# A fixed order for the first product of a decoder layer: small loads, transposes and splits placed by hand

## The chip, the cores and the metric

The kernel runs on one core of one Trainium2 chip. The metric is the device time of one execution in microseconds (us); the profile's span, from the first to the last instruction of the profiled execution, is a little shorter. Engines are named as the profile names them: PE (TensorE matmuls), PEld (its weight loads), DVE (VectorE), ACT (ScalarE), POOL (GpSimd), SP (SyncE, which here only issues DMAs).

## The reference: one layer of a hybrid trunk

For one sequence of 256 positions with 2048 channels, float32:

```
x = x + 1/2 * SwiGLU_1(RMSNorm(x))          # w_gate, w_up: 2048 x 5632, w_down: 5632 x 2048
x = x + mixer(RMSNorm(x))                   # three token mixers, w_in 2048 x 5120, w_out 2048 x 2048
x = x + 1/2 * SwiGLU_2(RMSNorm(x))
out = RMSNorm(x)
swiglu(h, wg, wu, wd) = (silu(h @ wg) * (h @ wu)) @ wd
```

## The kernel before

All large products run as three matmuls per block: the stationary operand is x (or h) transposed, split into a high and a low part in a reduced float32 format (`xh`, `xl`), the moving operand is a weight tile, split the same way (`wh`, `wl`), and PE sums hi·wh, lo·wh and hi·wl. The 256 positions are two tiles of 128 rows (t = 0, 1), the 2048 channels are 16 blocks k of 128, and outputs are made in columns of 512. So one k costs 6 matmuls of 512 columns, and one product over all 16 k costs 96. Weights come over SP's queue into `wt` (4 buffers, up to four k per load, 1 MB); ACT rounds `wt` to `wh`, DVE makes `wl = wt - wh` (3 buffers each).

The first product, `ag` (x times the first 512 columns of w_gate), is special, because x itself has to be brought in first. `first_block` (L528) runs ahead of each load of weights that begins a new group of four k: it loads the next 512 channels of x, PE turns them (`tp`, L230: 8 transposes of 128x128 into two banks of PSUM), and for each of the four k in it ACT writes `xh` (L252, with the norm's gain from `prm`) and DVE writes `xl` (L253), both reading `tp`. The loads of weights are cut 1, 1, 2, 4, 4, 4. `prm` comes from a small load and one transpose (`pp`, L87). At the very start 14 transposes of the identity (`spin`, L101) keep PE occupied while nothing has landed.

The order on each engine is not that of the text: a list scheduler, which works with a model of durations, places every instruction, and the weight splits of the ordinary `gemm` have a raised priority. The product `au` (the same x times w_up) follows `ag`.

Of the kernel before, what the change touches and what calls it, by code (L numbers as in the profile page):

```python
# [1 line left out]

# [6 lines left out]
F32 = mybir.dt.float32  # L9
F32R = mybir.dt.float32r  # L10
# [6 lines left out]
P = 128  # L17
NB = 512
# [6 lines left out]
def hybrid_trunk(ctx, tc, x, ffn1_norm, ffn1_w_gate, ffn1_w_up, ffn1_w_down, mix_norm, w_in,  # L25
# [31 lines left out]
    xr = [pool.tile([P, T, NB], F32, name=f"x{n}") for n in range(DN)]  # L57
    xv = x[0].rearrange("(t p) d -> p t d", p=P)

    def load_x(n):  # L60
        nc.sync.dma_start(out=xr[n], in_=xv[:, :, n * NB:(n + 1) * NB])


    small, col = [], {}
# [7 lines left out]
    NP = sum(r.shape[0] for r in small)  # L72
    prm = pool.tile([P, NP], F32, name="prm")

    def load_params(which, at):
        n = sum(r.shape[0] for r in which)
        rows = pool.tile([n, P], F32, name="rows", tag="rows", bufs=1)
        r0 = 0
        for v in which:
            nc.scalar.dma_start(out=rows[r0:r0 + v.shape[0], :], in_=v)  # L80
            r0 += v.shape[0]
        return rows, at, n

# [3 lines left out]
        nc.tensor.transpose(pp[:, :n], rows, ident[:n, :n])  # L87
        nc.vector.tensor_copy(out=prm[:, at:at + n], in_=pp[:, :n])

    first_params = load_params(small[:1], 0)  # L90
    load_x(0)
    ident = pool.tile([P, P], F32, name="ident")
    make_identity(nc, ident)
    mhalf = pool.tile([P, T], F32, name="mhalf")
# [1 line left out]

    early = pool.tile([P, T], F32, name="early")
    nc.scalar.activation(out=early, in_=mhalf, func=AF.Silu)
    spin = tp_tile("spin")
    for i in range(14):  # L100
        nc.tensor.transpose(spin[:, :P], ident, ident)  # L101
    place_params(first_params)

# [31 lines left out]


    high = [None]
    later = []  # L140

    def gemm(lhs, w, n0, ks, name, cuts=None, before=None, by_tile=None):

        def bank_pair():
            return psum.tile([P, T, NB], F32, name=name, tag="acc", bufs=2)

        acc = bank_pair()  # L150
        acc_of = [acc] * T
        if by_tile:
            acc_of = [acc] + [bank_pair() for _ in range(T - 1)]
        nk = len(ks)
        c0 = 0
        held = []

        def products(t, c0, kk, wh, wl):
            ts = slice(t * P, (t + 1) * P)
            for i, k in enumerate(kk):  # L160
                hi, lo = lhs(k)
                first, last = c0 + i == 0, c0 + i == nk - 1
                acc = acc_of[t]
                nc.tensor.matmul(acc_of[t][:, t, :], lhsT=hi[:, ts], rhs=wh[:, i, :], start=first, stop=False)  # L164
                nc.tensor.matmul(acc_of[t][:, t, :], lhsT=lo[:, ts], rhs=wh[:, i, :], start=False, stop=False)  # L165
                nc.tensor.matmul(acc_of[t][:, t, :], lhsT=hi[:, ts], rhs=wl[:, i, :], start=False, stop=last)  # L166

        cuts = cuts or [CH] * (nk // CH)
        for ci, m in enumerate(cuts):
            kk = ks[c0:c0 + m]  # L170
            if before:
                before(kk[0])
            wt = stat.tile([P, CH, NB], F32, name="wt", tag="wt", bufs=4)
            nc.sync.dma_start(
                out=wt[:, :m],
                in_=w[kk[0] * P:(kk[-1] + 1) * P, n0:n0 + NB].rearrange("(k p) n -> p k n", p=P))
            wh = stat.tile([P, CH, NB], F32R, name="wh", tag="wh", bufs=3)
            wl = stat.tile([P, CH, NB], F32R, name="wl", tag="wl", bufs=3)
            with nullcontext() if before else tc.high_priority():
                high[0] = nc.scalar.activation(out=wh[:, :m], in_=wt[:, :m], func=AF.Copy)  # L180
                nc.vector.tensor_sub(out=wl[:, :m], in0=wt[:, :m], in1=wh[:, :m].bitcast(F32))  # L181
            if by_tile and ci >= len(cuts) - 3:
                held.append((c0, kk, wh, wl))
            else:
                for i, k in enumerate(kk):
                    for t in range(T):
                        products(t, c0 + i, [k], wh[:, i:i + 1], wl[:, i:i + 1])
            c0 += m
            step()
        if by_tile:  # L190
            for t in range(T):
                for h in held:
                    products(t, *h)
                by_tile(t, acc_of[t])
        return acc
# [46 lines left out]
                                    in_=sv[a * Q:(a + 1) * Q, :, :, j, :])  # L242
        return dst

    def gained(n, c0, at_once=False):

        tp = transposed(xr[n]) if at_once else turned(xr[n], work([P, 4, S], "xt"))
        hi = stat.tile([P, 4, S], F32R, name="xh", tag="xh", bufs=4)
        lo = stat.tile([P, 4, S], F32R, name="xl", tag="xl", bufs=4)
        for i in range(4):  # L250
            g = prm[:, c0 + 4 * n + i:c0 + 4 * n + i + 1]
            nc.scalar.activation(out=hi[:, i, :], in_=tp[:, i, :], func=AF.Copy, scale=g)  # L252
            nc.vector.scalar_tensor_tensor(out=lo[:, i, :], in0=tp[:, i, :], scalar=g,  # L253
                                           in1=hi[:, i, :].bitcast(F32), op0=ALU.mult,
                                           op1=ALU.subtract)
        return hi, lo
# [16 lines left out]
                                           in1=xr[n][:, t, :], op0=ALU.mult, op1=ALU.add)  # L273


    def ffn(xt, rs, wg, wu, wd, after, cuts=None, before=None, last_tile=None):

        ht = {}  # L280

        def hidden(j, **first):
            ag = gemm(block_of(xt), wg, j * NB, range(KD), "ag", **first)
# [24 lines left out]
            later.append(turn)  # L308

        for j0 in range(0, FB, 6):  # L310
            js = range(j0, min(j0 + 6, FB))
            for j in js:
                hidden(j, **(dict(cuts=cuts, before=before) if j == 0 else {}))
            ks = range(4 * js[0], 4 * js[-1] + 4)
            done = js[-1] == FB - 1
            for n in range(DN):
                if done and n == DN - 1 and last_tile:
                    def tile_done(t, acc, n=n):
                        residual(acc, n, 0.5, [t])
                        last_tile(t)  # L320
                    gemm(block_of(ht), wd, n * NB, ks, "ad", by_tile=tile_done)
                    continue
                acc = gemm(block_of(ht), wd, n * NB, ks, "ad")
                residual(acc, n, 0.5)
                if done:
                    after(n)


    def mixer(l, xt, rs_of, after):
# [1 line left out]
        rs = rs_of()  # L331
        cc, cp = col["conv", l], col["ps", l]
        pw = pool.tile([P, 4, P], F32, name="pw", tag="pw", bufs=1)
        nc.scalar.dma_start(out=pw, in_=pool_w[l].rearrange("g c d -> c g d"))
        DA = D // 2
        off = {"q": 0, "k": DA, "v": 2 * DA, "b": 3 * DA, "c": 3 * DA + NB, "u": 3 * DA + 2 * NB,
               "p": 3 * DA + 3 * NB}
# [187 lines left out]

    ss0, xt, r0 = new_stats(), {}, []

    def first_block(k):  # L528
        if k % 4 == 0:
            n = k // 4  # L530
            if n:
                load_x(n)
            xt[n] = gained(n, col["ffn1", 0], at_once=True)

    def first_rs():
        if not r0:
            r0.append(rstd_of(ss0))
            more = load_params(small[1:], small[0].shape[0])
            later.extend([lambda: place_params(more), masks, pool_consts])
        return r0[0]  # L540

# [38 lines left out]

    rs = first_rs
    for l in range(DEPTH):
        start = dict(cuts=[1, 1, 2, 4, 4, 4], before=first_block) if l == 0 else {}
        x1, r1 = phase("mix", l, lambda a: ffn(xt, rs, ffn1_w_gate[l], ffn1_w_up[l], ffn1_w_down[l],
                                               a, **start))
# [36 lines left out]
```

## Time and profile before

| what | value |
|---|---|
| median of three runs | 1793.72 us (1793.63 to 1793.86) |
| the profiled execution's own time | 1793.22 us |
| its span | 1791.1 us |
| PE busy | 1776.9 us, 99% |
| DVE, ACT busy | 64%, 42% |
| first matmul of `ag` starts | 8.87 us |
| `ag` and `au` are both through, the next `ag` starts | 58.08 us |

PE is occupied nearly throughout, so the span is read as a chain of PE work, with the few stretches in which PE waits; those lie in the first 20 us. [...]

### The profile page before, as it was taken

The page shows a single profiled execution, that of the slowest core. Times are in us where ns is not written, and L with a number is a line of the kernel's source. Part 1 is how long each engine was busy: PE and PEld are TensorE (multiplying, and loading weights), DVE is VectorE, ACT ScalarE, POOL GpSimd, SP SyncE. Part 2 cuts the span into 40 slices and gives each one's busy share as a digit, 9 for nine tenths or more (in the row PEclk, how much of TensorE's full clock was granted, in tenths as well). Part 3 has the DMA queues.
Part 4 walks back from the last instruction along what each step waited for, and adds up shares of the span by engine and source line. Part 5 has one row for each costly group of instructions (what it writes and reads, how often), then busy time and mean ns, then how long its engine had stood idle before and what let it go on. Part 6 is the DMA issues. An engine that isn't in the chain of part 4 may idle for free.

```text
span 1791.1 us, 19137 instructions
## 1 busy us (share of the span) xinstructions
PE 1776.9 (99%) x7928; PEld 1464.4 (82%) x7928; DVE 1144.3 (64%) x1260; ACT 748.6 (42%) x598; POOL 5.5 (0%) x19
## 2 busy tenths in 40 slices
PE   8999999999999999999999999999999999999998
PEld 7888888888888888887778888888888888888886
DVE  5766666444666687768767896666664446666653
ACT  6434433333344344545544455443443334433342
POOL 0000000000000000000000000000000000000000
PEclk9999999999999999999999999999999999999999
DMA  8655555555555555554545555555556555555652
GB/s 289 211 189 196 199 192 188 190 201 196 188 190 198 198 181 195 197 199 146 188 141 188 167 207 190 188 188 194 198 197 209 189 189 196 199 191 188 218 197 78
DMA packets 172262, 342.32 MB, mean 191 GB/s; under 512 B 5456, under 2 KB 6032, under 8 KB 172176
## 3 DMA queue, kind: packets, MB, share of 16 engines
q1 hardware_dynamic: 171232, 339.76, 56.2%
q10 hardware_dynamic: 944, 1.34, 0.3%
q8 instruction: 62, 1.02, 0.2%
q14 instruction: 24, 0.20, 0.0%
HBM read 338.98 MB, written 2.10 MB: 190 GB/s over the span
## 4 chain that ended last, share of the span: by engine, by line
PE 98%; DVE 1%; DMA 0%; ACT 0%; issue 0%; ACTq 0%; POOLq 0%
PE au L164 9%; PE ad L166 9%; PE au L165 9%; PE ad L164 9%; PE au L166 9%; PE ad L165 9%; PE ag L166 9%; PE ag L164 9%; PE ag L165 9%; PE az L164 4%; PE az L166 4%; PE az L165 4%; PE ao L166 1%; PE ao L165 1%; PE ao L164 1%; DVE wl L181 0%
## 5 line engine op out<-in xcount | busy, mean ns | idle before, releaser
L181 DVE TENSOR_TENSOR wl<-wt,wh 128x2048 fp32r<-128x2048 f32 (+1 forms) x322 | 732.8, 2277 | 543.4 <-ACT wh L180 541.4
L180 ACT ACTIVATE wh<-wt 128x2048 fp32r<-128x2048 f32 (+1 forms) x322 | 613.6, 1905 | 867.0 <-PE au L165 281.3
L164 PE MATMUL ag<-wh,xh 128*128 128x512 f32 x704 | 274.8, 390 | 2.1 <-ACT xh L252 2.1
L165 PE MATMUL ag<-wh,xl 128*128 128x512 f32 x704 | 274.6, 390 | 0.3 <-DVE xl L253 0.3
L166 PE MATMUL ag<-wl,xh 128*128 128x512 f32 x704 | 274.5, 390 | 0.2 <-DVE wl L181 0.2
L164 PE MATMUL au<-wh,xh 128*128 128x512 f32 x704 | 274.0, 389 | 0.0
L165 PE MATMUL au<-wh,xl 128*128 128x512 f32 x704 | 273.9, 389 | 0.0
L166 PE MATMUL au<-wl,xh 128*128 128x512 f32 x704 | 273.9, 389 | 0.0
L165 PE MATMUL ad<-wh,hl 128*128 128x512 f32 x704 | 273.9, 389 | 0.0
L164 PE MATMUL ad<-wh,hh 128*128 128x512 f32 x704 | 273.9, 389 | 0.0
L166 PE MATMUL ad<-wl,hh 128*128 128x512 f32 x704 | 273.7, 389 | 0.0
L241 DVE STREAM_TRANSPOSE ht<-h 32x256 f32<-32x256 f32 x352 | 153.5, 436 | 5.6
L164 PEld LDWEIGHTS ag<-wh,xh 128*128 128x128 f32 x704 | 132.4, 188 | 29.7 <-ACT xh L252 2.4
L166 PEld LDWEIGHTS ag<-wl,xh 128*128 128x128 f32 x704 | 132.5, 188 | 28.0 <-DVE wl L181 0.6
L165 PEld LDWEIGHTS ag<-wh,xl 128*128 128x128 f32 x704 | 132.4, 188 | 28.1 <-DVE xl L253 0.8
L165 PEld LDWEIGHTS ad<-wh,hl 128*128 128x128 f32 x704 | 132.2, 188 | 27.5
L164 PEld LDWEIGHTS au<-wh,xh 128*128 128x128 f32 x704 | 132.2, 188 | 27.5
L166 PEld LDWEIGHTS au<-wl,xh 128*128 128x128 f32 x704 | 132.2, 188 | 27.4
L166 PEld LDWEIGHTS ad<-wl,hh 128*128 128x128 f32 x704 | 132.2, 188 | 27.4
L165 PEld LDWEIGHTS au<-wh,xl 128*128 128x128 f32 x704 | 132.2, 188 | 27.3
L164 PEld LDWEIGHTS ad<-wh,hh 128*128 128x128 f32 x704 | 132.2, 188 | 27.3
L164 PE MATMUL az<-wh,xh 128*128 128x512 f32 x320 | 126.8, 396 | 0.0
(116 smaller groups left out, 1142.1 us busy)
## 6 DMA issues: line engine op xcount, KB each, us to landing
wt<-in_ffn_w_up_dram SPq DMA_DIRECT2D x88, 1024.0 KB, 5.1
wt<-in_ffn_w_down_dram SPq DMA_DIRECT2D x88, 1024.0 KB, 5.1
wt<-in_ffn_w_gate_dram SPq DMA_DIRECT2D x87, 1024.0 KB, 5.1
wt<-in_w_in_dram SPq DMA_DIRECT2D x40, 1024.0 KB, 5.0
wt<-in_w_out_dram SPq DMA_DIRECT2D x16, 1024.0 KB, 5.1
x<-in_x_dram SPq DMA_DIRECT2D x4, 512.0 KB, 10.3
out_dram<-xg SPq DMA_DIRECT2D x8, 256.0 KB, 3.1
gf<-in_final_norm_dram ACTq DMA_DIRECT2D x2, 512.0 KB, 4.7
```

The costliest lines, as they stand in the source:

```text
L164: nc.tensor.matmul(acc_of[t][:, t, :], lhsT=hi[:, ts], rhs=wh[:, i, :], start=first, stop=False)
L165: nc.tensor.matmul(acc_of[t][:, t, :], lhsT=lo[:, ts], rhs=wh[:, i, :], start=False, stop=False)
L166: nc.tensor.matmul(acc_of[t][:, t, :], lhsT=hi[:, ts], rhs=wl[:, i, :], start=False, stop=last)
L180: high[0] = nc.scalar.activation(out=wh[:, :m], in_=wt[:, :m], func=AF.Copy)
L181: nc.vector.tensor_sub(out=wl[:, :m], in0=wt[:, :m], in1=wh[:, :m].bitcast(F32))
L241: nc.vector.transpose(out=dv[j * Q:(j + 1) * Q, :, :, a, :], in_=sv[a * Q:(a + 1) * Q, :, :, j, :])
```

## The change

The scheduler no longer orders the first product. A new function `opening` writes it out by hand, under a manual schedule:

- x comes in five loads (the first 512 channels as two halves), and the first product's weights in loads of one or two k, all in a written order; a further load is issued where a buffer comes free.
- The first 14 idle transposes are followed, after the transposes of the first half of the first x load, by five more.
- `prepare(n)` (8 transposes) and `ready(n)` (the four `xh`, `xl`) of x's block n stand ahead of the products of k = 4n - 1, and the split of the weights for k = 4n stands behind those products in the text.
- Within a k the two position tiles share each operand pair: hi·wh, hi·wh, lo·wh, lo·wh, hi·wl, hi·wl.
- Four small parameter loads move from ACT's queue to POOL's, and the load of `pw` (256 KB, for the mixer) from ACT's queue to SP's, behind the last load of the first FFN.

```
-    def load_x(n):
-        nc.sync.dma_start(out=xr[n], in_=xv[:, :, n * NB:(n + 1) * NB])
+    def load_x(n, c0=0, c1=NB):
+        nc.sync.dma_start(out=xr[n][:, :, c0:c1], in_=xv[:, :, n * NB + c0:n * NB + c1])
...
-    first_params = load_params(small[:1], 0)
-    load_x(0)
+    first_params = load_params(small[:1], 0, nc.scalar)
...
-    spin = tp_tile("spin")
-    for i in range(14):
-        nc.tensor.transpose(spin[:, :P], ident, ident)
-    place_params(first_params)
+
+    def spin(n):
+        dst = psum.tile([P, T, NB], F32, name="spin", tag="acc", bufs=2)
+        for i in range(n):
+            nc.tensor.transpose(dst[:, 0, :P], ident, ident)
...
+    def split_w(wt, m):
+        wh = stat.tile([P, CH, NB], F32R, name="wh", tag="wh", bufs=3)
+        wl = stat.tile([P, CH, NB], F32R, name="wl", tag="wl", bufs=3)
+        high[0] = nc.scalar.activation(out=wh[:, :m], in_=wt[:, :m], func=AF.Copy)
+        nc.vector.tensor_sub(out=wl[:, :m], in0=wt[:, :m], in1=wh[:, :m].bitcast(F32))
+        return wh, wl
+
+    def opening(xt, c0, w, name):
+
+        acc = psum.tile([P, T, NB], F32, name=name, tag="acc", bufs=2)
+        pieces = {}
+
+        def prepare(n, blocks):
+            if n not in pieces:
+                pieces[n] = tp_tile("tp").rearrange("p (k s) -> p k s", k=4)
+                xt[n] = split_tiles()
+            for i in blocks:
+                for t in range(T):
+                    nc.tensor.transpose(pieces[n][:, i, t * P:(t + 1) * P],
+                                        xr[n][:, t, i * P:(i + 1) * P], ident)
+            return n, blocks
+
+        def ready(n, blocks):
+            gain_split(pieces[n], xt[n], n, c0, blocks)
+
+        def products(k, wh, wl, i):
+            hi, lo = (v[:, k % 4, :] for v in xt[k // 4])
+            for a, b, at in ((hi, wh, 0), (lo, wh, 1), (hi, wl, 2)):
+                for t in range(T):
+                    nc.tensor.matmul(acc[:, t, :], lhsT=a[:, t * P:(t + 1) * P], rhs=b[:, i, :],
+                                     start=k == 0 and at == 0, stop=k == KD - 1 and at == 2)
+
+        H = NB // 2
+        load_x(0, 0, H)
+        ws = {0: load_w(w, 0, [0])}
+        load_x(0, H, NB)
+        ws[1] = load_w(w, 0, [1])
+        ws[2] = load_w(w, 0, [2, 3])
+        load_x(1)
+        ws[4] = load_w(w, 0, [4, 5])
+        spin(14)
+        place_params(first_params)
+        prepare(0, [0, 1])
+        spin(5)
+        ready(0, [0])
+        h0 = split_w(ws[0], 1)
+        ready(0, [1])
+        h1 = split_w(ws[1], 1)
+        products(0, *h0, 0)
+        prepare(0, [2, 3])
+        ready(0, [2, 3])
+        h2 = split_w(ws[2], 2)
+        products(1, *h1, 0)
+        products(2, *h2, 0)
+        for k in range(3, KD):
+
+            if k % 4 == 3 and k + 1 < KD:
+                n = (k + 1) // 4
+                ws[k + 3] = load_w(w, 0, [k + 3, k + 4])
+                if n + 1 < DN:
+                    load_x(n + 1)
+                    ws[k + 5] = load_w(w, 0, [k + 5, k + 6])
+                prepare(n, range(4))
+                ready(n, range(4))
+            if k % 2:
+                products(k, *h2, 1)
+                if k + 1 < KD:
+                    h2 = split_w(ws[k + 1], 2)
+            else:
+                products(k, *h2, 0)
+        return acc
...
-        nc.scalar.dma_start(out=pw, in_=pool_w[l].rearrange("g c d -> c g d"))
+        with tc.issue_after(loaded[0].ins):
+            nc.sync.dma_start(out=pw, in_=pool_w[l].rearrange("g c d -> c g d"))
...
+    def gain_split(tp, tiles, n, c0, blocks=range(4)):
+        hi, lo = tiles
+        for i in blocks:
             g = prm[:, c0 + 4 * n + i:c0 + 4 * n + i + 1]
             nc.scalar.activation(out=hi[:, i, :], in_=tp[:, i, :], func=AF.Copy, scale=g)
             nc.vector.scalar_tensor_tensor(out=lo[:, i, :], in0=tp[:, i, :], scalar=g,
...
+    def begin(wg):
+        with tc.manual_schedule():
+            return opening(xt, col["ffn1", 0], wg, "ag")
...
-            more = load_params(small[1:], small[0].shape[0])
+            more = load_params(small[1:], small[0].shape[0], nc.gpsimd)
```

What this makes of ACT's order: before, around the splits of x's first and second block (`xh_116` is block 0, `xh_178` block 1, `wh_190` the weights of k = 4 to 7), with the semaphores that each waits for:

```order
L180 ACTIVATE wh_152<-wt_150 128x1024
L80 DMA rows_460<-in_pool_scale_dram 4x128 [waits DMAHW6_49]
L252 ACTIVATE xh_116<-tp_107,prm_68 128x256 [waits DVE_49]
L252 ACTIVATE xh_178<-tp_169,prm_68 128x256 [waits PE_49]
L252 ACTIVATE xh_116<-tp_107,prm_68 128x256 [waits DVE_49]
L252 ACTIVATE xh_178<-tp_169,prm_68 128x256 [waits DVE_49]
L252 ACTIVATE xh_116<-tp_107,prm_68 128x256 [waits DVE_49]
L180 ACTIVATE wh_190<-wt_188 128x2048 [waits DMAHW7_49,Activation_49]
```

And now, at the same place (`xh_180` is block 1, `wh_204` the weights of k = 4 and 5, `wh_220` those of k = 6 and 7, `xh_236` block 2):

```order
L153 ACTIVATE wh_158<-wt_96 128x1024 [waits DMAHW5_49]
L328 ACTIVATE xh_180<-tp_179,prm_68 128x256 [waits PE_49]
L328 ACTIVATE xh_180<-tp_179,prm_68 128x256 [waits DVE_49] x3
L153 ACTIVATE wh_204<-wt_99 128x1024 [waits DMAHW7_49,Activation_49]
L153 ACTIVATE wh_220<-wt_174 128x1024 [waits DMAHW0_49,Activation_49]
L328 ACTIVATE xh_236<-tp_235,prm_68 128x256 [waits PE_49]
L328 ACTIVATE xh_236<-tp_235,prm_68 128x256 [waits DVE_49] x3
```

Before, splits of two blocks of x alternated; now the four of one block follow each other, each of the last three with a wait for DVE, and the weights of the block's first k stand behind all four.

On PE, before, the transposes of x's second block (`tp_169`) stood behind the products of k = 0 (`wh_128`), and eighteen matmuls (k = 1, 2, 3) came between them and the first use of that block:

```order
L164 MATMUL ag_106<-wh_128,xh_116 128x512
L165 MATMUL ag_106<-wh_128,xl_117 128x512
L166 MATMUL ag_106<-wl_129,xh_116 128x512
L230 MATMUL tp_169<-ident_72,x1_65 128x128 x8
L164 MATMUL ag_106<-wh_140,xh_116 128x512
L165 MATMUL ag_106<-wh_140,xl_117 128x512
L166 MATMUL ag_106<-wl_141,xh_116 128x512
```

Now (`tp_179` the second block's transposes, `wh_158` the weights of k = 2 and 3, `wh_204` with `xh_180` the first product of the second block, k = 4):

```order
L179 MATMUL ag_89<-wl_159,xh_120 128x512 x2
L168 MATMUL tp_179<-ident_71,x1_65 128x128 x8
L179 MATMUL ag_89<-wh_158,xh_120 128x512 x2
L179 MATMUL ag_89<-wh_158,xl_121 128x512 x2
L179 MATMUL ag_89<-wl_159,xh_120 128x512 x2
L179 MATMUL ag_89<-wh_204,xh_180 128x512 x2
L179 MATMUL ag_89<-wh_204,xl_181 128x512 x2
```

The transposes moved behind k = 2: six matmuls (k = 3) are left between them and the block's first use, and the same holds for the third and the fourth block of x.

## Rows read from the trace of the kernel before

**Rows 1.** The page: busy time by engine, and the chain that ended last.

```profile
PE 1776.9 (99%) x7928; PEld 1464.4 (82%) x7928; DVE 1144.3 (64%) x1260; ACT 748.6 (42%) x598; POOL 5.5 (0%) x19
PE 98%; DVE 1%; DMA 0%; ACT 0%; issue 0%; ACTq 0%; POOLq 0%
```

**Rows 2.** Stretches: length, busy us by engine, PEclk, DMA share, GB/s.

```profile
5.00:9.00 4.00, 1.19 (x9) 0.99 (x9) 0.98 (x3) 1.28 (x3) 0.00 (x0) 0.93 1.00 347
9.00:13.00 4.00, 4.00 (x15) 2.86 (x15) 2.38 (x4) 2.03 (x4) 0.00 (x0) 0.65 1.06 391
32.10:58.00 25.90, 25.90 (x115) 21.47 (x115) 12.84 (x10) 12.47 (x17) 1.20 (x3) 1.00 0.61 204
```

**Rows 3.** Timeline of PE: start, length, line, out<-in, idle before.

```profile
1.36 3.25 PE L101 MATMUL spin<-ident 128*128 128x128 f32 x14 [1.36 <-POOL ident masks.py:199]
5.69 1.06 PE L230 MATMUL tp<-ident,x 128*128 128x128 f32 x8 [0.76 <-DMA x<-in_x_dram]
8.87 0.80 PE L164 MATMUL ag<-wh,xh 128*128 128x512 f32 x1 [2.12 <-ACT xh L252]
10.41 0.63 PE L164 MATMUL ag<-wh,xh 128*128 128x512 f32 x1
10.83 0.63 PE L165 MATMUL ag<-wh,xl 128*128 128x512 f32 x1
17.31 1.03 PE L230 MATMUL tp<-ident,x 128*128 128x128 f32 x8
18.10 0.48 PE L164 MATMUL ag<-wh,xh 128*128 128x512 f32 x1
27.30 0.39 PE L165 MATMUL ag<-wh,xl 128*128 128x512 f32 x1
31.60 0.39 PE L166 MATMUL ag<-wl,xh 128*128 128x512 f32 x1
58.08 0.39 PE L164 MATMUL ag<-wh,xh 128*128 128x512 f32 x1
```

**Rows 4.** Timeline of ACT and of its queue in the opening.

```profile
7.91 0.33 ACTq L80 DMA_DIRECT2D rows<-in_ffn_norm_dram  x1
8.34 0.47 ACT L252 ACTIVATE xh<-tp,prm 128x256 fp32r<-128x256 f32 x1 [1.20 <-DMA pw<-in_pool_w_dram]
8.72 0.62 ACT L180 ACTIVATE wh<-wt 128x512 fp32r<-128x512 f32 x1
10.55 1.06 ACT L180 ACTIVATE wh<-wt 128x1024 fp32r<-128x1024 f32 x1 [1.22 <-DMA wt<-in_ffn_w_gate_dram]
18.38 0.47 ACT L252 ACTIVATE xh<-tp,prm 128x256 fp32r<-128x256 f32 x1 [1.42 <-PE tp L230]
```

**Rows 5.** Groups by form up to 36 us: the split's DVE side.

```profile
L253 DVE SCALAR_TENSOR_TENSOR xl<-tp,prm,xh 128x256 fp32r<-128x256 f32 x16 | 7.4, 480 | 1.3 <-ACT xh L252 1.0
L181 DVE TENSOR_TENSOR wl<-wt,wh 128x512 fp32r<-128x512 f32 x2 | 1.4, 691 | 2.1 <-ACT wh L180 2.0
L181 DVE TENSOR_TENSOR wl<-wt,wh 128x1024 fp32r<-128x1024 f32 x1 | 1.2, 1224 | 1.6 <-ACT wh L180 1.6
```

**Rows 6.** Timeline: two engines that split one PSUM tile, in the mixer and the opening.

```profile
945.36 0.47 ACT L465 ACTIVATE yh<-yp,prm 128x256 fp32r<-128x256 f32 x1 [2.81 <-PE yp L461]
945.87 0.48 DVE L466 SCALAR_TENSOR_TENSOR yl<-yp,prm,yh 128x256 fp32r<-128x256 f32 x1 [0.99 <-ACT yh L465]
946.38 0.47 ACT L465 ACTIVATE yh<-yp,prm 128x256 fp32r<-128x256 f32 x1 [0.55 <-DVE yl L466]
19.36 0.87 ACT L252 ACTIVATE xh<-tp,prm 128x256 fp32r<-128x256 f32 x2 [0.51 <-DVE xl L253]
```

**Rows 7.** DMA issues of the first 1.5 us: KB each, median us to landing.

```profile
x<-in_x_dram SPq DMA_DIRECT2D x1, 512.0 KB, 4.8
rows<-in_ffn_norm_dram ACTq DMA_DIRECT2D x1, 8.0 KB, 3.9
wt<-in_ffn_w_gate_dram SPq DMA_DIRECT2D x1, 256.0 KB, 5.3
```

More of the change, by code (lines that the diff above doesn't have):

```diff
@@ L1 @@
-from contextlib import ExitStack, nullcontext
+from contextlib import ExitStack
 import concourse.bass as bass
@@ L73, in hybrid_trunk, with load_params @@
     prm = pool.tile([P, NP], F32, name="prm")
-    def load_params(which, at):
+    def load_params(which, at, queue):
         n = sum(r.shape[0] for r in which)
@@ L79, in load_params @@
         for v in which:
-            nc.scalar.dma_start(out=rows[r0:r0 + v.shape[0], :], in_=v)
+            queue.dma_start(out=rows[r0:r0 + v.shape[0], :], in_=v)
             r0 += v.shape[0]
@@ L139, in hybrid_trunk, with load_w @@
     high = [None]
+    loaded = [None]
     later = []
-    def gemm(lhs, w, n0, ks, name, cuts=None, before=None, by_tile=None):
+    def load_w(w, n0, kk):
+        wt = stat.tile([P, CH, NB], F32, name="wt", tag="wt", bufs=4)
+        loaded[0] = nc.sync.dma_start(
+            out=wt[:, :len(kk)],
+            in_=w[kk[0] * P:(kk[-1] + 1) * P, n0:n0 + NB].rearrange("(k p) n -> p k n", p=P))
+        return wt
+    def split_w(wt, m):
[4 more added lines that the diff above has]
+        return wh, wl
@@ L147, in bank_pair, with gemm @@
+    def gemm(lhs, w, n0, ks, name, by_tile=None):
         def bank_pair():
@@ L166, in products @@
                 nc.tensor.matmul(acc_of[t][:, t, :], lhsT=hi[:, ts], rhs=wl[:, i, :], start=False, stop=last)
-        cuts = cuts or [CH] * (nk // CH)
+        cuts = [CH] * (nk // CH)
         for ci, m in enumerate(cuts):
             kk = ks[c0:c0 + m]
[L171 to L181, printed above, removed]
+            wt = load_w(w, n0, kk)
+            with tc.high_priority():
+                wh, wl = split_w(wt, m)
             if by_tile and ci >= len(cuts) - 3:
@@ L243, in turned, with split_tiles, gained @@
         return dst
[L245 to L250, printed above, removed]
+    def split_tiles():
+        return (stat.tile([P, 4, S], F32R, name="xh", tag="xh", bufs=4),
+                stat.tile([P, 4, S], F32R, name="xl", tag="xl", bufs=4))
+    def gained(n, c0):
+        return gain_split(turned(xr[n], work([P, 4, S], "xt")), split_tiles(), n, c0)
+    def gain_split(tp, tiles, n, c0, blocks=range(4)):
+        hi, lo = tiles
+        for i in blocks:
             g = prm[:, c0 + 4 * n + i:c0 + 4 * n + i + 1]
@@ L273, in residual, with ffn, hidden @@
                                            in1=xr[n][:, t, :], op0=ALU.mult, op1=ALU.add)
-    def ffn(xt, rs, wg, wu, wd, after, cuts=None, before=None, last_tile=None):
+    def ffn(xt, rs, wg, wu, wd, after, begin=None, last_tile=None):
         ht = {}
-        def hidden(j, **first):
-            ag = gemm(block_of(xt), wg, j * NB, range(KD), "ag", **first)
+        def hidden(j, first=None):
+            ag = first(wg) if first else gemm(block_of(xt), wg, j * NB, range(KD), "ag")
             if first:
@@ L312, in ffn @@
             for j in js:
-                hidden(j, **(dict(cuts=cuts, before=before) if j == 0 else {}))
+                hidden(j, begin if j == 0 else None)
             ks = range(4 * js[0], 4 * js[-1] + 4)
@@ L526, in hybrid_trunk @@
     ss0, xt, r0 = new_stats(), {}, []
[L528 to L533, printed above, removed]
+    def begin(wg):
+        with tc.manual_schedule():
+            return opening(xt, col["ffn1", 0], wg, "ag")
     def first_rs():
@@ L582, in hybrid_trunk @@
     for l in range(DEPTH):
-        start = dict(cuts=[1, 1, 2, 4, 4, 4], before=first_block) if l == 0 else {}
         x1, r1 = phase("mix", l, lambda a: ffn(xt, rs, ffn1_w_gate[l], ffn1_w_up[l], ffn1_w_down[l],
-                                               a, **start))
+                                               a, begin if l == 0 else None))
         x2, r2 = phase("ffn2", l, lambda a: mixer(l, x1, r1, a))
```

## The prediction, made before the run

> **What bounds the kernel now.** I read the busy times and the chain first [rows 1]: PE is busy for 99% and makes 98% of the chain, so time can be won or lost only where PE waits or where it runs at its lower clock level. The timeline of PE [rows 3] shows where that is: the first matmul of the first product starts at 8.87 us, after 2.12 us of idleness that the first `xh` ended. The stretches [rows 2] show what followed: from 5 to 9 us PE was busy for only 1.19 of 4 us, and the granted clock, full until then, fell. [...] From 32 us on PE is full and at full clock. A point behind the change at which both kernels have done the same work is the end of the second product, 192 matmuls: 58.08 us. At full clock without a wait those and three blocks of transposes (0.79 us each, 17.31 to 18.10) last 43.4 + 2.4 = 45.8 us; from 8.87 to 58.08 are 49.2. So 3.4 us of clock and waits are to be had behind the first matmul, and some more by an earlier start.
>
> **The change: an earlier start.** ACT gave the first `xh` at 8.34 us, after 1.20 us in which a DMA issue of its own queue stood in the way [rows 4]. That issue is gone from ACT, and `xh` no longer waits for 512 KB of x. The whole of x's first block took 4.8 us from issue to landing and 8 KB took 3.9 [rows 7], so the half, issued at 0.7, lands between 4.6 and 5.5; I take 4.9, nearer the small one, since little moves so early. The first weights, issued at 1.2 behind 512 KB, landed after 5.3 us, at 6.5; behind half of that I take 5.8 (between x's 5.5 and 6.5). Four transposes at 0.13 (1.06 for 8) end at 5.4; `xh` starts at 5.5, `wh` 0.38 later (8.34 to 8.72), takes 0.62, and the first matmul starts at 6.6 us. Bounds: 6.3 with the earliest landings, 7.2 with the latest. The five idle transposes (5 x 0.13 = 0.7 us) lie between the transposes and 6.6, where PE has nothing; without that cover they would cost these 0.7. They shorten the idle time ahead of the first matmul from 2.1 us to about 0.5, and I take it that the clock stays up there.
>
> **The change: x's splits in a row.** This is what decides. Where ACT and DVE split one PSUM tile block by block, the next ACT step waits for the DVE step before it: in the mixer 945.36, 945.87, 946.38 [rows 6], one block in 1.02 us; in the opening the same wait is named (0.51 us, until `xl`). Before, ACT's splits of two blocks of x alternated, which hid the wait. Now four of one block follow each other, and the order shows the wait on each of the last three. The first of the four starts 1.07 us after the transposes do (17.31 to 18.38), the fourth 3 x 1.02 = 3.06 later; `wh` of the next weights stands behind it: 0.38 to its start and 1.06 to its end [rows 4], and 0.05 to PE. So the first matmul of each new block (k = 4, 8, 12) starts 1.07 + 3.06 + 0.38 + 1.06 + 0.05 = 5.62 us after its transposes. PE meanwhile has the transposes, 0.79, and the six matmuls of k = 4n - 1, 6 x 0.2263 = 1.36: it is through at 2.15 and waits **3.47 us**, three times. Next late is `wl`: `wh`'s end + 0.03 + 1.22 [rows 5] + 0.05 = 6.87, while PE has done hi·wh and lo·wh (4 matmuls) at 6.53: 0.34 more. Two matmuls and the two k that follow (12 matmuls, whose weights ACT and DVE have split by then) end at 6.87 + 14 x 0.2263 = 10.04: the period of a block, against 24 x 0.2263 + 0.79 = 6.22 without waits.
>
> **The sum.** First matmul 6.6; k = 0 is through at 7.96 (its `wl`, 0.69 behind `wh`, is in time). The second half's transposes follow. Its two `xh` start at +0.68 (half the transposes, so 0.4 less than 1.07) and +1.70, `wh` at +2.08, PE goes on with k = 2 at +3.19, having done k = 1 at +1.76: 1.43 us of waiting. `wl` lets it on at +4.44, k = 2 ends at +4.9: 12.86 us. Two periods of 10.04 bring the third late block's transposes to 32.94; its first k ends 7.32 later, three more k take 4.07: the first product ends at 44.3. The second adds 96 x 0.2263 = 21.7: 66.0 us, **8.0 later** than 58.08.
>
> **The clock.** Three waits of 3.5 us without any PE work are each longer than the 2.12 us (with 0.76 before it) after which the clock fell [rows 2, 3]. A fall as long as that one, 3.4 us, lets PE do 8 matmuls in place of 15 and costs 15 x 0.2263 - 8 x 0.2263 = 1.6; part of it lies in the wait itself or under the 0.34 for `wl`. Per fall: no less than 0.7, no more than 1.6; I take 1.2, three times 3.6. The bounds of this term are 0 (no fall) and 4.8.
>
> **The rest.** The loads: x's second block, needed at 12.9, stands behind 1.5 MB, which at the opening's 350 to 390 GB/s [rows 2] is there at about 10 to 11; weights of k = 2 and 3 are needed at 10.0 and stand behind 1 MB (some 9; if they land with before's at 10.5, the sum grows by 0.5). Later ones have 10 us per block for 1.5 MB. SP's queue has nothing behind it that is near. Nothing in the trace shows a DMA issued by POOL: between 0.3 us (an issue on ACT's queue, at 7.91) and 1.2 (the idleness it left on ACT) each [rows 4], four issued from 5 us on are through by 10, and 3.9 us to landing [rows 7] make 14; the transpose that needs them stands behind k = 11, past 30 us, in a wait. `pw` on SP's queue is one issue among 1 MB loads that keep the DMA engines at 0.61 [rows 2], and is needed only near 945 us [rows 6]: nothing; without that slack the time of 256 KB at 391 GB/s, 0.7 us. The new order inside a k has the same six matmuls.
>
> Together 8.0 + 3.6 = 11.6 us on the profiled execution's own 1793.2 make 1804.8; the median of the runs is 0.5 above that execution: **1805 us**.
>
> [...] The last row of [rows 6] has an ACT step on one block waiting for DVE's step on the block before. [...]
>
> **Rivals.** Chances stand in brackets.
> - *Waits as worked out, clock up* (0.17): +8.0, **1801.2**. For it: here PE is full on both sides of each wait, and before its fall it was not. Against: 3.5 us is longer than what lowered it.
> - *Waits, clock down, first matmul no earlier* (0.06): the half loads land like whole ones and the start stays near 8.9: +2.3, **1807**. For it: many loads share the engines (DMA share 1.00 [rows 2]).
> - *The waits go by halves of the tile* (0.04): the third split starts 0.38 after the second, the fourth when the third's `xl` is done at 2 x 0.49 after the second's: 2.5 in place of 3.06, 3 x 0.56 = 1.7 less, **1803.1**. [...]
> - *Splits do not take turns* (0.07): ACT goes at 0.38 a block. The start of the fourth is 1.14 in place of 3.06, 5.8 less over three blocks and 0.6 in the first, and waits of 1.5 us may leave the clock up: 11.6 - 6.4 - 3.6 = +1.6, **1795**: no change that can be told.
> - *It does what it is written for* (0.03): the splits of x fit behind the six matmuls (ready at 2.15 and not 5.62) and no wait is left: 6.6 + 43.4 + 0.4 + 2.4 = 52.8, 5.3 less, **1788**. It decides for faster if the waits of a block sum to under 0.5 us (5.3 - 3.6 over three). Against it: the order puts `wh` behind all four `xh`.
>
> The forecast itself (waits, two or three falls of the clock) has 0.63, with 1802.5 to 1808 as its own range.
>
> **How the numbers follow.** About 0.2%, 3.6 us, is what a measurement of this kernel can tell from no change. Slower than that: 0.63 + 0.17 + 0.06 + 0.04 = 0.90; within: 0.07; faster: 0.03. The range runs from 1799.5 (clock up and the earliest start, with the first steps a little quicker) to 1809.5 (three falls of 1.6, the latest start, weights of k = 2 late), which leaves out about 2 in 10: the two rivals below it and the outer ends of the others.
>
> **What would show it.** In the changed kernel's timeline: the first matmul near 6.6 us at the higher level; ACT's four `xh` of a block about 1.0 us apart; PE waits of 3 to 4 us, ended by `wh`, ahead of k = 4, 8 and 12, and one of 1.4 ahead of k = 2; granted clock at one half in stretches that follow those waits; the second product through at 66 to 70 us, and from there on the same rows as before. The prediction is wrong if `xh` stand 0.4 apart, if `wh` of the next block is done before its `xh`, or if the clock never falls.

## The result and the profile after

The changed kernel takes **1807.03 us** (median of 5 runs, 1806.49 to 1807.32) where the kernel before, run beside it, takes 1793.63: 1.0074 of its time, 95% interval 1.0064 to 1.0085. The forecast was 1805.0 with a range of 1799.5 to 1809.5. The profiled execution took 1807.32, its span is 1805.5; it can be read against [rows 1 to 7].

The page first (busy time by engine, the chain): PE is busy for 6.8 us more than in [rows 1] although five transposes are all that it has to do in addition, and its share of the chain is 96% in place of 98%.

```profile
PE 1783.7 (99%) x7933; PEld 1468.3 (81%) x7933; DVE 1145.5 (63%) x1263; ACT 744.5 (41%) x585; POOL 7.7 (0%) x23
PE 96%; DVE 1%; issue 0%; ACT 0%; POOLq 0%; ACTq 0%
```

Selected rows of PE's timeline (start, length, line, out<-in, idle before) hold the whole difference:

```profile
4.76 1.11 PE L168 MATMUL tp<-ident,x 128*128 128x128 f32 x4
5.66 1.27 PE L102 MATMUL spin<-ident 128*128 128x128 f32 x5
6.96 0.78 PE L179 MATMUL ag<-wh,xh 128*128 128x512 f32 x2
11.63 0.73 PE L179 MATMUL ag<-wh,xh 128*128 128x512 f32 x2 [1.14 <-ACT wh L153]
12.20 0.62 PE L179 MATMUL ag<-wh,xl 128*128 128x512 f32 x2
13.46 1.04 PE L168 MATMUL tp<-ident,x 128*128 128x128 f32 x8
14.25 0.70 PE L179 MATMUL ag<-wh,xh 128*128 128x512 f32 x2
14.79 0.63 PE L179 MATMUL ag<-wh,xl 128*128 128x512 f32 x2
15.26 0.63 PE L179 MATMUL ag<-wl,xh 128*128 128x512 f32 x2
19.09 0.73 PE L179 MATMUL ag<-wh,xh 128*128 128x512 f32 x2 [3.20 <-ACT wh L153]
21.91 1.05 PE L179 MATMUL ag<-wh,xl 128*128 128x512 f32 x2
22.76 1.05 PE L179 MATMUL ag<-wl,xh 128*128 128x512 f32 x2
25.25 1.03 PE L168 MATMUL tp<-ident,x 128*128 128x128 f32 x8
30.88 1.15 PE L179 MATMUL ag<-wh,xh 128*128 128x512 f32 x2 [3.22 <-ACT wh L153]
36.69 1.04 PE L168 MATMUL tp<-ident,x 128*128 128x128 f32 x8
42.47 1.22 PE L179 MATMUL ag<-wh,xh 128*128 128x512 f32 x2 [3.17 <-ACT wh L153]
50.64 0.39 PE L243 MATMUL au<-wh,xh 128*128 128x512 f32 x1
72.40 0.39 PE L243 MATMUL ag<-wh,xh 128*128 128x512 f32 x1
```

The first matmul starts 1.9 us earlier than in [rows 3] (6.96 against 8.87). Then PE waits 1.14 us ahead of k = 2 and 3.20, 3.22 and 3.17 us ahead of k = 4, 8 and 12, each time for `wh`. The second product is through at 72.40 us, 14.3 later than 58.08; the spans differ by 14.4. So nothing behind it moved the time, the four parameter loads and `pw` included.

The stretches (length, busy us of PE, PEld, DVE, ACT, POOL, then PEclk, the granted share of PE's clock, DMA share, GB/s), the opening first, which answers to [rows 2], then the three in which the granted clock is at the lower level:

```profile
5.00:9.00 4.00, 3.98 (x20) 3.27 (x20) 2.15 (x5) 2.10 (x4) 2.17 (x4) 1.00 0.79 285
9.00:13.00 4.00, 2.79 (x12) 1.66 (x11) 2.35 (x4) 1.90 (x3) 0.00 (x0) 1.00 1.03 387
20.75:24.20 3.45, 3.45 (x10) 2.68 (x9) 0.68 (x1) 0.00 (x0) 0.00 (x0) 0.51 0.73 218
31.00:34.40 3.40, 3.40 (x9) 2.63 (x10) 2.22 (x2) 0.77 (x1) 0.00 (x0) 0.50 0.30 66
41.25:48.05 6.80, 5.58 (x13) 4.42 (x14) 5.14 (x4) 5.43 (x7) 0.00 (x0) 0.50 0.46 156
```

The fall that [rows 2] show in the opening is gone; three others have come, after each of the long waits, and the third lasts twice as long as the first two. Inside one, two matmuls take 0.85 us (21.91 to 22.76), outside 0.47 (14.79 to 15.26).

What PE waited for stands in the timelines of ACT and DVE:

```profile
14.53 0.47 ACT L328 ACTIVATE xh<-tp,prm 128x256 fp32r<-128x256 f32 x1 [2.95 <-PE tp L168]
15.56 0.47 ACT L328 ACTIVATE xh<-tp,prm 128x256 fp32r<-128x256 f32 x1 [0.55 <-DVE xl L329]
16.59 0.47 ACT L328 ACTIVATE xh<-tp,prm 128x256 fp32r<-128x256 f32 x1 [0.55 <-DVE xl L329]
17.61 0.47 ACT L328 ACTIVATE xh<-tp,prm 128x256 fp32r<-128x256 f32 x1 [0.55 <-DVE xl L329]
17.99 2.00 ACT L153 ACTIVATE wh<-wt 128x1024 fp32r<-128x1024 f32 x2
15.04 0.48 DVE L329 SCALAR_TENSOR_TENSOR xl<-tp,prm,xh 128x256 fp32r<-128x256 f32 x1 [2.20 <-ACT xh L328]
```

ACT and DVE take turns on `tp`: `xh` at 14.53, 15.56, 16.59, 17.61, each `xl` between two of them, 1.03 us a block as in [rows 6]; only then `wh`, which is what k = 4 lacks. The third `xh` waits 0.55 us for DVE as the second does, although it reads the other half of the tile: in this program the waits go by tile.

DMA issues of the first 2 us (KB each, median us to landing), against [rows 7]: the half loads of x and the first weights land sooner after their issue.

```profile
x<-in_x_dram SPq DMA_DIRECT2D x2, 256.0 KB, 3.9
wt<-in_ffn_w_gate_dram SPq DMA_DIRECT2D x1, 256.0 KB, 3.7
```

### The profile page after: what moved, and what is told of

The parts are those of the page before. It is cut to its first block, busy times and chain, and to the rows that moved or that the text cites. A ratio compares the mean times of both kernels' runs of the same rounds, so it can differ in the third digit from the quotient of the medians.

```text
span 1805.5 us, 19154 instructions
## 1 busy us (share of the span) xinstructions
PE 1783.7 (99%) x7933; PEld 1468.3 (81%) x7933; DVE 1145.5 (63%) x1263; ACT 744.5 (41%) x585; POOL 7.7 (0%) x23
## 3 DMA queue, kind: packets, MB, share of 16 engines
q8 instruction: 62, 1.02, 0.2%
## 4 chain that ended last, share of the span: by engine, by line
PE 96%; DVE 1%; issue 0%; ACT 0%; POOLq 0%; ACTq 0%
PE ad L245 9%; PE au L244 9%; PE au L243 9%; PE au L245 9%; PE ad L243 9%; PE ad L244 9%; PE ag L244 8%; PE ag L243 8%; PE ag L245 8%; PE az L243 4%; PE az L245 4%; PE az L244 4%; PE ao L245 1%; PE ao L244 1%; PE ao L243 1%; PE ag L179 0%
## 5 line engine op out<-in xcount | busy, mean ns | idle before, releaser
L154 DVE TENSOR_TENSOR wl<-wt,wh 128x2048 fp32r<-128x2048 f32 (+2 forms) x325 | 733.3, 2258 | 537.4 <-ACT wh L153 535.5
L153 ACT ACTIVATE wh<-wt 128x2048 fp32r<-128x2048 f32 (+2 forms) x325 | 613.7, 1890 | 862.1 <-PE au L244 278.7
L243 PE MATMUL ag<-wh,xh 128*128 128x512 f32 x672 | 261.4, 389 | 0.0
L244 PE MATMUL ag<-wh,xl 128*128 128x512 f32 x672 | 261.4, 389 | 0.0
L245 PE MATMUL ag<-wl,xh 128*128 128x512 f32 x672 | 261.4, 389 | 0.0
L243 PEld LDWEIGHTS ag<-wh,xh 128*128 128x128 f32 x672 | 126.1, 188 | 26.2
L245 PEld LDWEIGHTS ag<-wl,xh 128*128 128x128 f32 x672 | 126.1, 188 | 26.2
L244 PEld LDWEIGHTS ag<-wh,xl 128*128 128x128 f32 x672 | 126.1, 188 | 26.2
```

## The experiments

The theory: the loss is made of waits ahead of k = 4, 8 and 12, because `wh` stands behind four `xh` that take turns with DVE on one tile, and of the clock that falls after them. The rivals: the turns alone or the place of the weights alone make the waits; the clock plays no part; the loss is elsewhere, in the moved loads, the five idle transposes or x's halves.

**Weights first.** The changed kernel with the splits of the weights of k + 1 and k + 3 issued ahead of the transposes and the splits of x:

```
+                ahead[k + 1] = split_w(ws[k + 1], 2)
+                ahead[k + 3] = split_w(ws[k + 3], 2)
                 prepare(n, range(4))
                 ready(n, range(4))
...
-                    h2 = split_w(ws[k + 1], 2)
+                    h2 = ahead[k + 1]
```

> The weight splits for k = 4n to 4n + 3 stand ahead of the transposes and splits of x's block n; all else as in the changed kernel. If the place of the weights' split behind the four x splits makes the waits (the prediction's step), the three waits of 3.2 us ahead of k = 4, 8 and 12 go, and with them the falls of the clock: the first product ends some 15 us earlier, 1790.5 to 1793.5 us (up to 1.5 us of waiting may be left in the last block, where splits for the second product come in between). If late loads make the waits (rival), the waits stay and only their releaser has another name: 1807. If ACT and DVE taking turns is enough for the wait, with the weights' split anywhere, half is left: about 1800.

Measured: 1793.33 us (1793.04 to 1793.75), 0.9999 of the kernel before (0.999 to 1.0008). The four `xh` of a block still take turns, but PE hardly waits for them (0.2 us, once). The main waits of PE behind the first matmul, up to 70 us (us in total, times, longest), for the changed kernel and then for this one:

```profile
PE ag L179 <- ACT wh L153: 10.7, 4, 3.2
```

```profile
PE ag L179 <- ACT wh L153: 1.1, 1, 1.1
PE au L247 <- DVE wl L154: 0.9, 2, 0.6
```

So it is enough to take the weights' split out from behind the splits of x for the loss to go, turns or not. The granted clock is 1.00 from 5 us on in every stretch. The wait of 1.14 ahead of k = 2 is still there and 0.9 us of new ones, for splits of the second product's weights that stand behind those of the last block, came in; these eat what the earlier start and the full clock gave: the second product is through at 58.55 us, where the kernel before has 58.08.

**Two tiles.** The weights stay where the change puts them, but each of the blocks of x behind the first uses two PSUM tiles, split in the order 0, 2, 1, 3, so that ACT and DVE are on different tiles:

```
+                a = tp_tile("tp").rearrange("p (k s) -> p k s", k=4)
+                b = tp_tile("tp").rearrange("p (k s) -> p k s", k=4) if n else a
+                pieces[n] = [a, a, b, b]
...
-                ready(n, range(4))
+                ready(n, (0, 2, 1, 3))
```

> Blocks 1 to 3 of x are turned into two PSUM tiles each (channels 0 and 1, 2 and 3) and split in the order 0, 2, 1, 3, so that ACT has work in the other tile while DVE is in the first; the weights' split stays behind. If turn-taking on one tile is what spaces the x splits by 1.03 us, the fourth starts 1.5 us earlier: waits of about 1.7 us in place of 3.2, and 1802 us if the clock still falls as often, 1797 to 1798 if it stays up. If turn-taking costs nothing (DVE's or ACT's own speed spaces them), the splits stay 1 us apart and the time is 1807.

Measured: 1795.85 us (1795.26 to 1796.09), 1.0012 (1.0003 to 1.0022). ACT's timeline, then PE's, at the second block:

```profile
13.43 1.94 ACT L331 ACTIVATE xh<-tp,prm 128x256 fp32r<-128x256 f32 x4 [2.52 <-PE tp L170]
12.79 1.03 PE L170 MATMUL tp<-ident,x 128*128 128x128 f32 x8
16.36 0.73 PE L182 MATMUL ag<-wh,xh 128*128 128x512 f32 x2 [1.15 <-ACT wh L153]
```

The four `xh` now stand in one row, 0.49 apart, with no wait for DVE. The first starts 0.64 us after the transposes do and not 1.07, since it needs only the four transposes of its own tile; that is more than I had counted on. k = 4 starts 3.57 us after its transposes, not 5.63. PE waits 1.15 us ahead of k = 4, 1.16 ahead of k = 8 and 0.92 in two parts ahead of k = 12, and the clock does not fall (granted clock 1.00 in every stretch from 5 to 51 us). Of the loss of 13.4 us some 2 are left without any move of the weights: the turns on one tile and the place of `wh` behind them are one chain, and it breaks at either link.

**Waits filled.** The changed kernel with 24 idle transposes behind the products of k = 3, 7 and 11, where PE would wait:

```
                 products(k, *h2, 1)
+                if k % 4 == 3 and k + 1 < KD:
+                    spin(24)
```

> 24 idle transposes of the identity stand behind the products of k = 3, 7 and 11, in the three waits; nothing else changes. At full clock they take some 2.6 us, inside the wait. If the falls of the clock are due to PE standing idle, the clock stays up, the waits' ends stay where they are, and the 5 us that the lower level costs come back: 1802 us. If transposes do not keep the clock up, it falls as before, and the transposes, at 0.21 us each, outlast the wait: 1808 to 1813. If the clock's part of the loss is nothing, 1807.

Measured: 1802.0 us (1801.83 to 1802.11), 1.0047 (1.0032 to 1.0062), 5.0 us less than the changed kernel. PE's timeline shows that the dependent work did not come sooner:

```profile
13.17 1.04 PE L173 MATMUL tp<-ident,x 128*128 128x128 f32 x8
15.43 2.78 PE L165 MATMUL fill<-ident 128*128 128x128 f32 x24
18.80 0.73 PE L184 MATMUL ag<-wh,xh 128*128 128x512 f32 x2 [0.58 <-ACT wh L153]
```

k = 4 stands 5.63 us behind its transposes as before. What changed is the pace behind it. The stretches from the first matmul of k = 4, 8 and 12 to the end of the last one before PE turns to other work, in the changed kernel and then here:

```profile
19.09:25.25 6.16, 6.10 (x18) 4.50 (x19) 2.34 (x2) 0.90 (x1) 0.00 (x0) 0.72 0.52 164
30.88:36.69 5.81, 5.81 (x19) 4.58 (x20) 2.34 (x2) 0.89 (x1) 0.00 (x0) 0.71 0.58 190
42.47:50.64 8.17, 8.17 (x24) 6.52 (x25) 6.19 (x4) 6.09 (x8) 0.00 (x0) 0.66 0.70 253
```

```profile
18.80:23.41 4.61, 4.55 (x19) 3.36 (x19) 2.34 (x2) 0.90 (x1) 0.00 (x0) 1.00 0.42 125
29.03:33.61 4.58, 4.51 (x19) 3.36 (x19) 2.35 (x2) 0.90 (x1) 0.00 (x0) 1.00 0.47 148
39.23:45.16 5.93, 5.86 (x24) 4.54 (x25) 5.41 (x4) 5.74 (x7) 0.00 (x0) 1.00 0.59 199
```

The same matmuls (18, 18 and 24) take 1.55, 1.23 and 2.24 us longer at the lower clock, 5.0 together. This is the clock's whole share. In the waits PE had nothing but transposes (128x128 float32, 24 in 2.78 us, then 0.58 idle), and the granted clock behind them is 1.00 where it is 0.72, 0.71 and 0.66 in the changed kernel: in this form transposes alone kept it up.

**One k earlier.** Transposes and splits of x's next block moved ahead of the products of k = 4n - 2, so that twelve matmuls in place of six cover them:

```
-            if k % 4 == 3 and k + 1 < KD:
...
+            if k % 4 == 2 and k + 2 < KD:
+                n = (k + 2) // 4
                 prepare(n, range(4))
                 ready(n, range(4))
```

(For k = 2 the two calls stand ahead of its products in the straight part.)

> Transposes and splits of x's blocks 1 to 3 stand one k earlier (ahead of k = 4n - 2 in place of 4n - 1); the weights' split stays behind them. By the prediction's sum the wait is 5.6 us less what PE has to do meanwhile, so each of the three waits shrinks by one k, 1.36 us, to about 1.9: 1803 us if the clock falls as often, 1798 if it stays up at such waits. If a load ends the waits, the place of the transposes changes nothing: 1807.

Measured: 1799.18 us (1797.86 to 1801.13), 1.003 (1.0017 to 1.0042). Waits of 1.79, 1.84 and 1.46 us are left: six matmuls more cover 1.36, and the longer waits went down by about that. In the profiled run they still let the clock fall, three times: the granted clock is 0.86 from 13 to 25 us, 0.86 from 25 to 37 and 0.88 from 37 to 51. The first of these stretches:

```profile
13.00:25.00 12.00, 9.84 (x38) 7.09 (x36) 5.24 (x8) 4.33 (x8) 0.00 (x0) 0.86 0.63 219
```

That run, 1801.13, is the slowest of the six, with a mean clock of 0.995; the others took 1797.86 to 1799.92 at 0.997 to 0.998. Their falls are not shown by a trace; times near the 1798 that was estimated for a clock that stays up, and the higher mean clock, speak for fewer or shorter ones.

**The loads alone.** The kernel before, with nothing but the parameter loads on POOL's queue and `pw` on SP's:

```
-            nc.scalar.dma_start(out=rows[r0:r0 + v.shape[0], :], in_=v)
+            queue.dma_start(out=rows[r0:r0 + v.shape[0], :], in_=v)
...
-        nc.scalar.dma_start(out=pw, in_=pool_w[l].rearrange("g c d -> c g d"))
+        with tc.issue_after(loaded[0].ins):
+            nc.sync.dma_start(out=pw, in_=pool_w[l].rearrange("g c d -> c g d"))
```

> One part alone: the kernel before, in which only the parameter loads go to POOL's queue and pw's load to SP's. The scheduler now puts the splits of the first two weights ahead of the first x split on ACT. If the DMA issues on ACT's queue held the first matmul (the prediction's 1.2 us), it starts 0.3 to 1.2 us earlier than 8.87, and the time is 1792.5 to 1793.5 us; if the first x split waits for the second weights instead, nothing is won: 1793.6 or a little more.

Measured: 1792.83 us (1792.28 to 1793.31), 0.9997 (0.9988 to 1.0005). The first matmul comes 1.04 us earlier, and of that 0.57 is left at the end of the second product (57.51 against 58.08):

```profile
7.83 0.50 PE L165 MATMUL ag<-wh,xh 128*128 128x512 f32 x1 [1.25 <-ACT xh L253]
57.51 0.39 PE L165 MATMUL ag<-wh,xh 128*128 128x512 f32 x1
```

So moving the loads, with the order on ACT that the scheduler then makes, costs nothing, and without the halves of x it gives half of the earlier start; a gain in time is not shown, the interval holds 1.

**No five idle transposes.**

```
         prepare(0, [0, 1])
-        spin(5)
```

> The changed kernel without the five idle transposes. They lie in front of the first matmul, where PE has nothing to do, so its start stays at 6.3 to 7.0 us. If they keep the clock up (the prediction's reading), it falls at some 8 us as before and the products of k = 0 to 2 take up to 1.6 us longer, of which the wait ahead of k = 2 hides about 1: 1807 to 1808. If they do nothing, 1807; if they stand in the way of the first matmul, 1806.5.

Measured: 1807.1 us (1804.0 to 1808.78), 1.0074 (1.0061 to 1.0086): the median of the changed kernel, with a wider spread. In the profiled run, the fastest of the five (its span is 1802.2), the first matmul starts at 6.25 after a wait of 1.08 us, the granted clock is 1.00 from 5 to 13 us, and only two of the three long waits are followed by a fall: the granted clock is 0.86 from 13 to 25 us and 0.88 from 37 to 51, but 1.00 from 25 to 37, and the block behind the second wait runs at full pace (pairs 0.45 to 0.47 us apart from 31.27 on).

```profile
29.45 0.73 PE L179 MATMUL ag<-wh,xh 128*128 128x512 f32 x2 [3.21 <-ACT wh L153]
30.02 0.63 PE L179 MATMUL ag<-wh,xl 128*128 128x512 f32 x2
```

The five transposes show no effect on the median; the spread goes with the mean clock: 0.996 and 0.998 in the two runs under 1805, 0.995 in the three above 1807.

**x's first block in one load.**

```
-        load_x(0, 0, H)
+        load_x(0)
...
-        load_x(0, H, NB)
```

> The changed kernel with x's first block in one load of 512 KB, as before. By the prediction's sum the halves bring the first transposes some 0.6 us forward and the whole chain behind them with it: 1807.3 to 1808. If the first weights' landing or the second half sets the pace, nothing changes: 1807.0.

Measured: 1809.63 us (1809.44 to 1809.96), 1.009 (1.0075 to 1.0106): the halves are worth 2.6 us, more than I expected.

```profile
5.64 1.12 PE L168 MATMUL tp<-ident,x 128*128 128x128 f32 x4 [0.81 <-DMA x<-in_x_dram]
7.83 1.22 PE L179 MATMUL ag<-wh,xh 128*128 128x512 f32 x2
8.86 0.92 PE L179 MATMUL ag<-wh,xl 128*128 128x512 f32 x2
13.20 0.73 PE L179 MATMUL ag<-wh,xh 128*128 128x512 f32 x2 [1.14 <-ACT wh L153]
```

The stretch in which the first pairs begin (columns as before):

```profile
5.00:9.00 4.00, 3.35 (x12) 2.76 (x13) 1.71 (x5) 1.98 (x4) 2.17 (x4) 1.00 1.02 394
```

The transposes begin 0.88 later, and so does the first matmul (7.83 against 6.96). But the first two pairs also run slower (1.03 us for the first, 7.83 to 8.86, in place of 0.62), and k = 2 is 1.57 late. The first takes as long as the pair at 42.47 in the changed kernel, 1.02 us at a granted clock of 0.50, yet the granted clock of this stretch is 1.00, as it is from 9 to 13 us, so what slowed them stays open. The rest is a longer low stretch behind k = 4 (granted clock 0.78 from 13 to 25 us, 0.86 in the changed kernel): k = 8 is 2.37 late (33.25 against 30.88), although its wait has the same length.

**Both edits.** Weights first and two tiles together.

> The changed kernel with the weights' splits ahead and with two PSUM tiles for each of x's blocks 1 to 3. If the waits ahead of k = 4, 8 and 12 were all that the written order lost, none of them is left, the early start at 6.3 to 7.0 us stays, and the second product is through at 54.5 to 57 us against 58.1 of before: 1790 to 1792.5 us, ahead of both kernels by a little (the wait of about 1 us ahead of k = 2 and some 0.1 us at each first matmul behind a wait remain). If the interleaving of the second product's splits with the last block's, seen with the weights ahead, costs as much as the order won, it is 1793 to 1794.

Measured: 1791.45 us (1790.92 to 1792.35), 0.9988 (0.998 to 0.9997). The second product is through at 56.81 us, and the granted clock is 1.00 from 5 us on; the wait ahead of k = 2 is left, and 0.56 us at k = 4.

**Both edits, tuned.** In addition the split of the weights of k = 2 and 3 goes ahead of `xh` of the blocks 2 and 3, and for x's second block alone the split for k = 6 behind its `xh`; the version with both edits was run once more beside it.

```
+        h2 = split_w(ws[2], 2)
         prepare(0, [2, 3])
         ready(0, [2, 3])
-        h2 = split_w(ws[2], 2)
...
+                if n > 1:
+                    ahead[k + 3] = split_w(ws[k + 3], 2)
...
+                if n == 1:
+                    ahead[k + 3] = split_w(ws[k + 3], 2)
```

> The version with the weights' splits ahead and two tiles per block still had two small waits: 1.14 us ahead of k = 2 (the split of that pair of weights stands behind xh of the blocks 2 and 3) and 0.56 us at k = 4 behind xl, where the split of the weights of k = 6 and 7 stands ahead of that block's xh. This version puts the first pair's split ahead of those xh, and, for the second block of x alone, the later pair's split behind them. Theory (the waits are there because of the order on ACT and DVE): the first falls from 1.14 to under 0.3, since its wh needs 1.06 us from the landing of its weights near 6.9 us and PE comes to k = 2 near 11; the second falls to under 0.1; together 1.0 to 1.6 us less: 1789.9 to 1790.5 us where the other version has 1791.45. Rival 1 (what stands ahead sets the pace: xh of the blocks 2 and 3 are late instead, by the 1.06 us that the weights' split now takes ahead of them): the wait only changes its name, 1791.2 to 1791.7. Rival 2 (the later pair, k = 6, is late in place of k = 4): the first wait goes, another of 0.5 to 1 us comes at k = 6: 1790.5 to 1791.2.

> The version with both edits once more, as the yardstick of the one beside it on the same chip: 1791.4 us (1790.9 to 1792.4 in the earlier runs), 0.9988 of the kernel before; if it is over 1792.5 or within 0.3 us of the kernel before, the gain of both edits is not held.

Measured: 1790.2 us (1789.73 to 1790.9), 0.9982 of the kernel before (0.9973 to 0.9991); both edits alone again 1791.0 (1790.7 to 1791.83), 0.9987 (0.9978 to 0.9996). PE's waits behind the first matmul, up to 70 us, are these in the tuned version:

```profile
PE ag L182 <- DVE xl L337: 0.3, 1, 0.3
```

Its second product is through at 54.77 us, where the kernel before has 58.08: 3.3 of the 3.4 us that the runs show. The wait ahead of k = 2 went because its `wh` now runs as soon as its weights have landed (at 8.41 us, 0.47 us of idleness ended by their load); that `xh` of the blocks 2 and 3 are late instead costs 0.3. So the order on ACT, not the landings, had made the 1.14. The wait of 0.56 at k = 4 is gone too, but it does not show in the profile of the second time that both edits ran either, so the gain over both edits, 0.8 us between the two medians, is put down to k = 2 alone. This version is 16.8 us under the changed kernel and 3.4 under the one before, with an interval that leaves out 1 but reaches to 0.9991.

## Why the prediction was right, and where its sizes were off

**The mechanism is shown.** The transposes of a block lead to its first product 5.63 us later for k = 4 and 8 (forecast 5.62), by the steps that were named: 1.07 to the first `xh`, three turns with DVE, `wh`. Taking away either the turns (two tiles) or what stands behind them (weights first) removes the falls of the clock and all or nearly all of the loss (1795.85 and 1793.33). The rival in which the waits go by halves of the tile is refuted by the third `xh` at 16.59, 1.03 after the second, where that rival has 0.38.

**The start.** Forecast 6.6, measured 6.96; the landing was sooner than taken (3.5 us after the issue at 0.74, so near 4.2, where 4.9 was taken), and the transposes begin at 4.76, straight behind other work of PE; but four of them took 0.90 us (4.76 to 5.66) in place of 0.53. In the variants with the same loads the start lies between 6.25 and 6.96, and it goes with these transposes: where they took 0.32 or 0.33 (4.76 to 5.09) it is 6.32 to 6.34, where they took 0.70 (4.76 to 5.46) it is 6.71. The granted clock is 1.00 in all of these, so why their pace differs stays open, and that 6.6 lies in the middle is in part luck. The five idle transposes were credited with keeping the clock up here; the run without them, at 1.00 from 5 to 13 us, shows that they were not needed.

**The waits.** Forecast 3.47 three times and 1.43; measured 3.17 to 3.22 and 1.14. The long ones are shorter by 0.25 because PE comes to them later (through at 15.89 by its row, 2.43 behind the transposes, and not 2.15), while the interval from transposes to product, which alone sets the time, is as forecast. What I left out is that a pair of matmuls behind a wait or behind transposes takes 0.54 to 0.57 us in place of 0.45 (14.25 to 14.79, 11.63 to 12.20). From the first matmul to the second block's transposes are 6.50 us, forecast 6.26; from k = 4 and k = 8 to the next transposes 4.61 and 4.58 with the clock up, forecast 4.42; behind k = 12 5.93, forecast 5.77; and for k = 12 the way from transposes to product is 5.78 (36.69 to 42.47), since DVE copies the late parameters between two `xl` (0.21 us at 39.34) and the third `xh` comes 0.15 later, a step that the prediction put at nothing. Together these add 0.9.

**The clock is the term that was mis-sized:** "I take 1.2, three times 3.6", with 1.6 as the most for one fall. No run shows the 1.2: it is an estimate between two bounds, and the runs show 5.0 in place of 3.6, made of 1.55, 1.23 and 2.24. The first two are inside the bounds given for a fall; the third is not, because I took all falls to be as long as the 3.4 us of the kernel before, and this one lasted 6.8, of which 5.6 with PE at work. What the 1.6 was worked out from is shown: in the kernel before the granted clock is 0.50 from 8.5 to 11.5 us, with 0.92 and 0.66 in the half microseconds on either side, which makes 3.4 us at half; a matmul took 0.42 us there (10.41 to 10.83) and 0.2263 later (27.30 to 31.60 in 19 steps) [rows 3], and the 96 of the second product here, 50.64 to 72.40, took 0.2267 each. The bound for all three, 4.8, was too low by 0.2.

**The sum.** Forecast +11.6 on the span; +0.36 for the start, +0.9 for first steps, +1.4 for the clock make 14.3, and 14.4 was measured. The median lies 13.4 above that of before, since the profiled execution of before was one of its quicker ones and that of after its slowest.

**The rivals.** *Clock up*, 1801.2: refuted by the granted clock, 0.50 or 0.51 in three stretches; the run with filled waits, which makes that case real, gives 1802.0. *Start no earlier*: refuted, 6.96. *Splits do not take turns*, 1795: not this kernel, but the run with two tiles, which makes it so for three of the four blocks, gives 1795.85; that it is so near is in part luck, since there the first block still takes turns and the first `xh` of the others comes 0.43 sooner. *It does what it is written for*, 1788: no variant comes to it; the best has 1790.2.

**The rest of the change at nothing** is borne out: the loads on other queues do not cost time (1792.83 where only they are moved). Not tried is how the change would stand with its own order of the six matmuls inside a k undone.

## What to carry to other kernels

Before one writes an order by hand, follow for each block the chain from its first dependent step to the matmul that needs it (here 5.63 us) and set it against the work that lies between (here 2.15); what is missing is paid once a block (3.2 us), and again where the clock falls after the wait (1.23 to 2.24). In an order written by hand put first what is ready and early in need (the weights' split), then what waits for others; and where two engines read the same PSUM tile, try two tiles, since here they took turns on one (1.03 us a block, 0.49 with two). A wait that can't be removed can be filled with idle transposes; here that kept the granted clock at 1.00 (1802.0 us in place of 1807.0).

## What the runs showed of the hardware that I had not expected

- Idle transposes of 128x128 float32 kept the clock up here: with 2.8 us of them in each 3.2 us wait the granted clock stayed at 1.00 (0.66 to 0.72 in the same blocks without them).
- Equal waits are not followed by equal falls: after waits of 3.2 us the low stretches of the changed kernel lasted 3.4, 3.4 and 6.8 us, and one such wait in the run without the five transposes was followed by none; the waits of 1.46 to 1.84 us in the profile with the splits one k earlier were followed by falls, those of 1.03 to 1.16 us in the other variants of the changed kernel by none. In the kernel before with only the loads moved the clock fell after two waits of 0.68 and 1.25 us with transposes between them (granted clock 0.64 from 9 to 13 us). So the length of a wait alone does not tell here whether a fall follows, or how long it lasts; what else decides stays open.
- The five idle transposes took 1.27 us in some profiles and 0.71 in others, while the granted clock from 5 to 9 us is 1.00 in both. So in these first microseconds the column does not tell the pace.
- Cutting the first load of x from 512 KB to two of 256 KB brought the first matmul forward by 0.9 us and the end by 2.6; the rest is the slower pace of the first two pairs and the longer low stretch behind k = 4 with the whole load, for which no run shows the reason.
